# Stick-breaking attention from running sums of weights, with masks on TensorE and a later forget gate

## The chip, the cores and the metric

One core of a Trainium2 chip runs the whole layer. The metric is the device time of one execution in microseconds. TensorE (PE) multiplies matrices, VectorE (DVE) and ScalarE (ACT) work element by element and read PSUM, GpSimd (POOL) works on SBUF and issues a few DMAs, and SyncE (SP) issues the loads.

## What is computed

One decoder layer for 512 tokens of width 1024 in float32: adaLN modulation, an input projection, two attention branches of 8 heads (head dimension 64) on the same input, gated merge, output projection, LayerNorm, then an MLP with a causal convolution and a second LayerNorm. The part that matters here:

```python
def _stick_breaking_attention(q, k, v):
    ...
        z = jnp.einsum('bhqd,bhkd->bhqk', qi, k).astype(jnp.float32) * ATTN_SCALE
        strict = kpos[None, :] < qpos[:, None]
        log_beta = jax.nn.log_sigmoid(z)
        log_one_minus = jnp.where(strict, jax.nn.log_sigmoid(-z), 0.0)
        rest = lax.cumsum(log_one_minus, axis=3, reverse=True) - log_one_minus
        a = jnp.where(strict, jnp.exp(log_beta + rest), 0.0)
        return jnp.einsum('bhqk,bhkd->bhqd', a.astype(v.dtype), v)
...
        log_f = jax.nn.log_sigmoid((f_a + b_forget).astype(jnp.float32)).transpose(0, 2, 1)
```

So the weight of key s for query t is A[t,s] = sigmoid(z[t,s]) times the product of sigmoid(-z[t,j]) over s < j < t, and zero for s >= t. The forgetting branch is a softmax with the running sum of log_f added to the scores.

## The kernel before

Every float32 operand of a matmul is split into a high part (`hi_of`, an ACT copy that rounds, line 75) and a low part (`lo_of`, a DVE subtraction, line 78), and every product is three matmuls of 128 x 512 (lines 116 to 118, 270, 411 to 413, 428 to 430).

The first stage, up to about 50 us, streams w_ada and the first columns of w_in and leaves q and k of the first pair of stick-breaking heads, the first gates and the forget logits in PSUM. `forget_evac` takes the logits out at once; `forget` later makes their log-sigmoid (Abs, Exp, Ln on ACT, lines 324 to 326), sums it with a scan on DVE (line 328), splits it into `chi` and sends rows of it by POOL DMAs into the score operands `s2` and `m2` of the forgetting heads (`decay_rows`, lines 342 and 343).

The second stage is the attention, which the change edits. A list `stream` holds generators of filler matmuls: projections of q and k for later pairs (`proj`), of v for the stick-breaking heads (`vproj`) and for the forgetting heads (`vgroup`), gates and branch projections. `fill(n)` takes the next n matmuls out of it, `fill_to(mark)` takes them up to a mark, and `lim` says how far they may be taken. Their weights are `items`: SP loads each 512 KB item into one of four `raw` buffers (line 132), two items ahead of use they are split. Between the weights stand the `ada` items (`add_ada`, `ada_proc`): the rest of the modulation, done by DVE alone (lines 561 and 566 for the first eight, line 170 for the later ones); `ada_split` and `ada_sum` (lines 584 and 585) sum groups of them over the partitions with TensorE.

16 heads, the 8 stick-breaking ones first, pass three stages. `stage_a` makes the scores of four query blocks with lines 454 and 455 in three PSUM banks, then the weights; `stage_b` turns the weights with TensorE (line 514) and splits them into `ph` and `pl`; `stage_c` multiplies them with v (line 532). Step n of the loop runs stage_a of head n+2, stage_b of head n+1 and stage_c of head n, with 9 filler matmuls between each. Before an even n the q and k projections of the next pair are taken in full; `q_evac` and `k_evac` take them out of PSUM into s1, s2, m1 and m2. Before n = 6 the marks make the four v groups and the projections of pair 4 run in one row. For a forgetting head, stage_a adds the mask `mska` to the diagonal blocks with a matmul (line 460). For a stick-breaking head, ACT makes `om` = sigmoid(-z) and `pt` = sigmoid(z) (lines 487 and 488), POOL sets the masked part of pt to zero (line 490), DVE scans the running product of om from the right, held at 1 in the masked part by the constant `one` (line 493), and POOL multiplies pt by it (line 494).

The instructions of each engine but SP are put in order when the program is built, by a planner that follows the written order as a priority, puts ready work ahead of work that its own cost model has waiting, and hands out the buffers; `tc.issue_after` adds an order on one engine. At run time each engine follows its order. Later stages (output projection, LayerNorm, MLP) are not edited.

Of the kernel before, what the change touches and what calls it, by code (L numbers as in the profile page):

```python
# [45 lines left out]
def layer_kernel(ctx: ExitStack, tc: tile.TileContext, out, xT, x, cT, crow, wa0, wa1, bcol, bgt, w1, wct, wv, bf,  # L46
# [21 lines left out]
    def const(shape, dt, s):  # L68
        return cons.tile(shape, dt, name=s, tag=s)
# [32 lines left out]
    G.memset(zerob, 0.0)  # L102
    mska = const([P, P], BF16, "mska")
    G.affine_select(mska, zerob, pattern=[[-1, P]], compare_op=ALU.is_ge, fill=NEG, base=0, channel_multiplier=1)
    one = const([P, 512], F32, "one")
    G.memset(one, 0.0)
    G.affine_select(one[:, 384:512], one[:, 384:512], pattern=[[-1, P]], compare_op=ALU.is_gt, fill=1.0, base=0, channel_multiplier=1)
    bfs = const([NH, 1], F32, "bfs")
    modc = const([P, 4, KT], F32, "modc")
    modr = const([P, 4, KT, 2], F32, "modr")  # L110
# [29 lines left out]
    def process():  # L140
        it = items[state["proc"]]
        if state["proc"] < EARLY:
            with tc.issue_after(state["after"].ins):
                it[4] = it[1](it[3])
        else:
            it[4] = it[1](it[3])
        state["proc"] += 1
# [208 lines left out]
    def q_evac(br, p, ps):  # L356
        for hh in range(2):
            h = 2 * p + hh
            r = slice(64 * hh, 64 * hh + 64)
            s1 = z(F32R, "s1")  # L360
            hi_of(s1[0:64, :], ps[r, :], 0.125)
            V.scalar_tensor_tensor(s1[64:128, :], ps[r, :], 0.125, fl(s1[0:64, :]), ALU.mult, ALU.subtract)
            d = hd.setdefault((br, h), {})
            d["s1"] = s1
            if br == 0:
                s2 = s2t[slot_free(idx(br, h))]
                hi_of(s2[0:64, :], ps[r, :], 0.125)
                d["s2"] = s2
            else:
                d["s2"] = s1  # L370

    def k_evac(br, p, ps):
        for hh in range(2):
            h = 2 * p + hh
            r = slice(64 * hh, 64 * hh + 64)
            m1 = z(F32R, "m1")
            hi_of(m1[0:64, :], ps[r, :])
            hi_of(m1[64:128, :], ps[r, :])
            m2 = m2t[slot_free(idx(br, h))]
            lo_of(m2[0:64, :], ps[r, :], m1[0:64, :])  # L380
            d = hd.setdefault((br, h), {})
            d["m1"], d["m2"] = m1, m2

    def v_evac(br, j, half, ps):
        vv = z(F32R, "vv")
# [19 lines left out]
    def vproj(br, j, last):  # L405
        ps = bank()
        weights(last)
        tb = slice(j * P, (j + 1) * P)
        for k in range(KT):
            h, l = items[wvi[k // 2]][4][k % 2]  # L410
            PE.matmul(ps, uh[k][:, tb], h, start=k == 0, stop=False)
            PE.matmul(ps, uh[k][:, tb], l, start=False, stop=False)
            PE.matmul(ps, ul[k][:, tb], h, start=False, stop=k == KT - 1)
            yield 3
        for half in range(2):
            v_evac(br, j, half, ps)

    vbk = []

# [25 lines left out]

    def stage_a(br, h):
        d = hd[(br, h)]
        bk = [bank(), bank(), bank()]

        def scores(i):  # L450
            b, o = OFS[i]
            w = max(256, (i + 1) * P)
            tb = slice(i * P, (i + 1) * P)
            PE.matmul(bk[b][:, o : o + w], d["s1"][:, tb], d["m1"][:, 0:w], start=True, stop=False)  # L454
            PE.matmul(bk[b][:, o : o + w], d["s2"][0:68, tb], d["m2"][0:68, 0:w], start=False, stop=br == 1)

        def mask(i):
            b, o = OFS[i]
            if br == 0:
                PE.matmul(bk[b][:, o + i * P : o + i * P + P], identb, mska, start=False, stop=True)  # L460

        scores(0)
        mask(0)
# [19 lines left out]
        else:  # L483
            for b in (0, 2, 1):
                w = SEG[b][-1][1]
                om = z(F32, "om")
                S.activation(om[:, 0:w], bk[b][:, 0:w], AF.Sigmoid, scale=-1.0)
                d["last"] = S.activation(pt[b][:, 0:w], bk[b][:, 0:w], AF.Sigmoid)
                dg = pt[b].rearrange("p (a c) -> p a c", c=P)[:, (0, 3, 1)[b] : w // P : 3, :]
                G.affine_select(dg, dg, pattern=[[0, dg.shape[1]], [-1, P]], compare_op=ALU.is_gt, fill=0.0, base=0, channel_multiplier=1)  # L490
                for s, e in SEG[b]:
                    d0 = om[:, s + 1 : e][:, ::-1]
                    V.tensor_tensor_scan(d0, d0, one[:, 513 - (e - s) : 512][:, ::-1], 1.0, ALU.mult, ALU.max)  # L493
                    G.tensor_tensor(pt[b][:, s : e - 1], pt[b][:, s : e - 1], om[:, s + 1 : e], ALU.mult)  # L494
        d["pt"] = pt
        scored.add(idx(br, h))
        if br == 0 and h + 4 < NH:
# [139 lines left out]
    stream, sums = [], []  # L637
    adas = [0]

    skip = [7]  # L640

    def add_ada(n=1):
        for _ in range(n):
# [42 lines left out]
    for p, ng in ((1, 0), (2, 0), (3, 2), (4, 1)):  # L686
        if p == 4:
            marks["v0"] = len(stream)
            for j in range(4):
                stream.append((vgroup, (j, add_item(wv[0, j], split_proc))))  # L690
                add_ada(2)
        add_pair(p)
        if p == 1:
            for j in range(4):
# [86 lines left out]
    heads = [(br, 2 * p + e) for br, p in seq for e in range(2)]  # L781
    last = hd[heads[1]]['last']
    for n, (b, h) in enumerate(heads):
        if n == 4:
            forget(last)
        f1, f2, f3 = FILL[n // 8]
        if n + 2 < 16:
# [9 lines left out]
        fill(f2)  # L797
        if n == 0:
            fill_to(marks["v1"])
        stage_c(b, h)  # L800
        if n == 7:
            lim[0] = marks["y0"]
# [291 lines left out]
```

## Time and profile before

| | |
|---|---|
| runs (us) | 770.62, 772.75, 772.47; median 772.47 |
| profiled execution | 773.12 us, its span 771.4 us |
| mean granted TensorE clock | 0.994 |
| busy | PE 98%, DVE 71%, ACT 45%, POOL 26% of the span |
| attention | about 50 to 310 us of the span, its stick-breaking heads up to about 200 us |

A row of a timeline gives the start in us, the length in us, the engine, the line of the kernel, the operation and its tiles as out<-in with the shape, and in brackets the idle time of the engine before it with what ended it. A row of a group of instructions gives their count, their busy time in us, the mean ns of one, and the idle time before them. Matmuls overlap: the step from one 512-column matmul to the next is 0.23 us though each shows 0.39.

### The profile page before, as it was taken

The page shows a single profiled execution, that of the slowest core. Times are in us where ns is not written, and L with a number is a line of the kernel's source. Part 1 is how long each engine was busy: PE and PEld are TensorE (multiplying, and loading weights), DVE is VectorE, ACT ScalarE, POOL GpSimd, SP SyncE. Part 2 cuts the span into 40 slices and gives each one's busy share as a digit, 9 for nine tenths or more (in the row PEclk, how much of TensorE's full clock was granted, in tenths as well). Part 3 has the DMA queues.
Part 4 walks back from the last instruction along what each step waited for, and adds up shares of the span by engine and source line. Part 5 has one row for each costly group of instructions (what it writes and reads, how often), then busy time and mean ns, then how long its engine had stood idle before and what let it go on. Part 6 is the DMA issues. An engine that isn't in the chain of part 4 may idle for free.

```text
span 771.4 us, 9543 instructions
## 1 busy us (share of the span) xinstructions
PE 752.7 (98%) x3538; PEld 622.3 (81%) x3538; DVE 546.5 (71%) x816; ACT 350.9 (45%) x587; POOL 197.9 (26%) x162
## 2 busy tenths in 40 slices
PE   8999999898999999999999999999999999999995
PEld 4877888786888888888889888888888888888885
DVE  6868668988789885776676787677656665534666
ACT  3568468725867555433145434444444433222300
POOL 1037236920100011363000780000000043945500
PEclk9999999999999999999999999999999999999999
DMA  8952310378332323455302524344332214322302
GB/s 330 405 181 82 110 56 28 111 243 274 112 113 92 121 86 123 155 166 163 137 1 71 204 76 146 119 178 137 112 106 93 100 54 165 122 96 88 105 27 83
DMA packets 31106, 99.68 MB, mean 129 GB/s; under 512 B 4274, under 2 KB 4786, under 8 KB 31059
## 3 DMA queue, kind: packets, MB, share of 16 engines
q1 hardware_dynamic: 30258, 98.72, 37.3%
q8 instruction: 28, 0.46, 0.3%
q10 hardware_dynamic: 288, 0.28, 0.1%
q0 software_dynamic: 512, 0.07, 0.1%
q14 instruction: 20, 0.16, 0.1%
HBM read 96.88 MB, written 2.10 MB: 128 GB/s over the span
## 4 chain that ended last, share of the span: by engine, by line
PE 83%; DVE 7%; ACT 5%; DMA 3%; issue 2%; DVEq 0%; ACTq 0%
PE ps L116 16%; PE ps L117 16%; PE ps L118 16%; PE ps L985 5%; PE ps L986 5%; PE ps L984 5%; PE ps L270 4%; PE ps L532 2%; PE ps L864 2%; PE ps L863 2%; PE ps L865 2%; PE ps L514 2%; DVE wl L78 1%; PE ps L454 1%; DVE om L493 1%
## 5 line engine op out<-in xcount | busy, mean ns | idle before, releaser
L78 DVE TENSOR_TENSOR wl<-raw,wh 128x1024 fp32r<-128x1024 f32 (+2 forms) x106 | 147.1, 1389 | 92.4 <-ACT wh L75 91.9
L75 ACT ACTIVATE wh<-raw 128x1024 fp32r<-128x1024 f32 (+2 forms) x106 | 110.3, 1042 | 98.7 <-PE ps L986 38.3
L116 PE MATMUL ps<-u2h,wh 128*128 128x512 f32 (+1 forms) x376 | 141.4, 376 | 0.0
L117 PE MATMUL ps<-u2l,wh 128*128 128x512 f32 (+1 forms) x376 | 141.3, 376 | 0.0
L118 PE MATMUL ps<-u2h,wl 128*128 128x512 f32 (+1 forms) x376 | 141.3, 376 | 0.0
L624 POOL TENSOR_TENSOR raw<-raw,gt 128x1024 f32<-128x1024 f32 x22 | 59.7, 2727 | 190.8 <-DVE gt L587 157.7
L117 PEld LDWEIGHTS ps<-u2l,wh 128*128 128x128 f32 x376 | 70.8, 188 | 12.9
L116 PEld LDWEIGHTS ps<-u2h,wh 128*128 128x128 f32 x376 | 70.8, 188 | 12.8
L118 PEld LDWEIGHTS ps<-u2h,wl 128*128 128x128 f32 x376 | 70.8, 188 | 12.6
L116 PE MATMUL ps<-uh,wh 128*128 128x512 f32 x200 | 79.7, 399 | 0.0
L117 PE MATMUL ps<-ul,wh 128*128 128x512 f32 x200 | 78.5, 392 | 0.0
L118 PE MATMUL ps<-uh,wl 128*128 128x512 f32 x200 | 78.4, 392 | 0.0
L985 PE MATMUL ps<-wl,hh 128*128 128x512 f32 x128 | 49.9, 390 | 0.0
L986 PE MATMUL ps<-wh,hl 128*128 128x512 f32 x128 | 49.8, 389 | 0.0
L984 PE MATMUL ps<-wh,hh 128*128 128x512 f32 x128 | 49.8, 389 | 0.0
L118 PEld LDWEIGHTS ps<-uh,wl 128*128 128x128 f32 x200 | 37.7, 189 | 8.1
L116 PEld LDWEIGHTS ps<-uh,wh 128*128 128x128 f32 x200 | 37.8, 189 | 7.1
L117 PEld LDWEIGHTS ps<-ul,wh 128*128 128x128 f32 x200 | 37.9, 189 | 6.9
L75 ACT ACTIVATE hh<-cv 128x512 fp32r<-128x512 f32 x22 | 13.9, 632 | 59.8 <-DVE cv L964 59.8
L612 POOL TENSOR_TENSOR raw<-raw,gt 128x1024 f32<-128x1024 f32 x8 | 19.9, 2498 | 78.2 <-DMA raw<-in_wo 47.2
L963 ACT ACTIVATE cv<-cv 128x512 f32<-128x512 f32 x22 | 13.9, 632 | 54.6 <-DVE cv L958 54.6
L494 POOL TENSOR_TENSOR pt<-pt,om 128x127 f32<-128x127 f32 (+3 forms) x32 | 34.5, 1088 | 1.8
(192 smaller groups left out, 1532.3 us busy)
## 6 DMA issues: line engine op xcount, KB each, us to landing
raw<-in_wup SPq DMA_DIRECT2D x44, 512.0 KB, 3.3
raw<-in_wa SPq DMA_DIRECT2D x32, 512.0 KB, 3.4
raw<-in_wct SPq DMA_DIRECT2D x25, 512.0 KB, 4.0
raw<-in_wdn SPq DMA_DIRECT2D x22, 512.0 KB, 3.3
wa<-in_wa SPq DMA_DIRECT2D x14, 512.0 KB, 7.9
raw<-in_wv SPq DMA_DIRECT2D x8, 512.0 KB, 3.9
raw<-in_wp SPq DMA_DIRECT2D x8, 512.0 KB, 3.4
raw<-in_wo SPq DMA_DIRECT2D x8, 512.0 KB, 3.2
```

Of the source, the lines that this page charges most:

```text
L75: S.activation(o, i, AF.Copy, scale=scale)
L78: return V.tensor_tensor(o, i, fl(hi), ALU.subtract)
L116: PE.matmul(ps, wh, ah, start=first, stop=False)
L117: PE.matmul(ps, wh, al, start=False, stop=False)
L118: PE.matmul(ps, wl, ah, start=False, stop=last)
L270: PE.matmul(grp[g], w, u, start=j == 0 and n == 0, stop=j == KT - 1 and n == (1 if g == 7 else 2))
L494: G.tensor_tensor(pt[b][:, s : e - 1], pt[b][:, s : e - 1], om[:, s + 1 : e], ALU.mult)
L612: G.tensor_tensor(r, r, gt[0], ALU.mult)
L624: G.tensor_tensor(r, r, gt[1], ALU.mult)
L984: PE.matmul(ps, hh[j][:, tb], w[0], start=first, stop=False)
L985: PE.matmul(ps, hh[j][:, tb], w[1], start=False, stop=False)
L986: PE.matmul(ps, hl[j][:, tb], w[0], start=False, stop=last)
```

## The change

The sum of A[t,s] v[s] over s is summed by parts. With R[t,s] the sum of the weights from s to t, it equals the sum over s of R[t,s] (v[s] - v[s-1]), v[-1] being zero. R comes from one scan from the right, R[s] = sigmoid(-z[s]) R[s+1] + sigmoid(z[s]), which is written into pt. The masked part gets its zero weights from TensorE, which adds -1e30 to the diagonal scores. POOL's masking and product of the stick-breaking heads are dropped.

- `v_diff` takes a block of v out of PSUM, shifts it down by one row with POOL DMAs (the row across the blocks alone, the other 127 together), subtracts, and splits the difference.
- `q_evac` and `k_evac` do the high parts of both heads first, then the low parts of both.
- The second weight split of the attention stage follows the low parts of k on each engine, no longer the last split of the first stage.
- The ada items start after two skipped places in place of seven, and one in place of two stands at each v group.
- `forget` is written at n = 6, not 4; 15 filler matmuls more stand before stage_c of head 0.

```diff
@@ -102,9 +102,8 @@
     G.memset(zerob, 0.0)
     mska = const([P, P], BF16, "mska")
     G.affine_select(mska, zerob, pattern=[[-1, P]], compare_op=ALU.is_ge, fill=NEG, base=0, channel_multiplier=1)
-    one = const([P, 512], F32, "one")
-    G.memset(one, 0.0)
-    G.affine_select(one[:, 384:512], one[:, 384:512], pattern=[[-1, P]], compare_op=ALU.is_gt, fill=1.0, base=0, channel_multiplier=1)
+    mskb = const([P, P], BF16, "mskb")
+    G.affine_select(mskb, zerob, pattern=[[-1, P]], compare_op=ALU.is_gt, fill=NEG, base=0, channel_multiplier=1)
     bfs = const([NH, 1], F32, "bfs")
     modc = const([P, 4, KT], F32, "modc")
     modr = const([P, 4, KT, 2], F32, "modr")
@@ -140,7 +139,7 @@
     def process():
         it = items[state["proc"]]
         if state["proc"] < EARLY:
-            with tc.issue_after(state["after"].ins):
+            with tc.issue_after(state["k" if state["proc"] else "after"].ins):
                 it[4] = it[1](it[3])
         else:
             it[4] = it[1](it[3])
@@ -359,7 +358,6 @@
             r = slice(64 * hh, 64 * hh + 64)
             s1 = z(F32R, "s1")
             hi_of(s1[0:64, :], ps[r, :], 0.125)
-            V.scalar_tensor_tensor(s1[64:128, :], ps[r, :], 0.125, fl(s1[0:64, :]), ALU.mult, ALU.subtract)
             d = hd.setdefault((br, h), {})
             d["s1"] = s1
             if br == 0:
@@ -368,6 +366,10 @@
                 d["s2"] = s2
             else:
                 d["s2"] = s1
+        for hh in range(2):
+            r = slice(64 * hh, 64 * hh + 64)
+            s1 = hd[(br, 2 * p + hh)]["s1"]
+            V.scalar_tensor_tensor(s1[64:128, :], ps[r, :], 0.125, fl(s1[0:64, :]), ALU.mult, ALU.subtract)
 
     def k_evac(br, p, ps):
         for hh in range(2):
@@ -376,10 +378,27 @@
             m1 = z(F32R, "m1")
             hi_of(m1[0:64, :], ps[r, :])
             hi_of(m1[64:128, :], ps[r, :])
-            m2 = m2t[slot_free(idx(br, h))]
-            lo_of(m2[0:64, :], ps[r, :], m1[0:64, :])
             d = hd.setdefault((br, h), {})
-            d["m1"], d["m2"] = m1, m2
+            d["m1"], d["m2"] = m1, m2t[slot_free(idx(br, h))]
+        for hh in range(2):
+            r = slice(64 * hh, 64 * hh + 64)
+            d = hd[(br, 2 * p + hh)]
+            state["k"] = lo_of(d["m2"][0:64, :], ps[r, :], d["m1"][0:64, :])
+
+    vfs = []
+
+    def v_diff(j, ps):
+        vf, dv = z(F32, "vf"), z(F32, "dv")
+        S.activation(vf, ps, AF.Copy)
+        if j == 0:
+            G.memset(dv[0:1, :], 0.0)
+        else:
+            G.dma_start(dv[0:1, :], vfs[-1][P - 1 : P, :])
+        G.dma_start(dv[1:P, :], vf[0 : P - 1, :])
+        vfs.append(vf)
+        V.tensor_tensor(dv, vf, dv, ALU.subtract)
+        for half in range(2):
+            v_evac(1, j, half, dv)
 
     def v_evac(br, j, half, ps):
         vv = z(F32R, "vv")
@@ -412,8 +431,7 @@
             PE.matmul(ps, uh[k][:, tb], l, start=False, stop=False)
             PE.matmul(ps, ul[k][:, tb], h, start=False, stop=k == KT - 1)
             yield 3
-        for half in range(2):
-            v_evac(br, j, half, ps)
+        v_diff(j, ps)
 
     vbk = []
 
@@ -445,6 +463,7 @@
 
     def stage_a(br, h):
         d = hd[(br, h)]
+        msk = mska if br == 0 else mskb
         bk = [bank(), bank(), bank()]
 
         def scores(i):
@@ -452,12 +471,11 @@
             w = max(256, (i + 1) * P)
             tb = slice(i * P, (i + 1) * P)
             PE.matmul(bk[b][:, o : o + w], d["s1"][:, tb], d["m1"][:, 0:w], start=True, stop=False)
-            PE.matmul(bk[b][:, o : o + w], d["s2"][0:68, tb], d["m2"][0:68, 0:w], start=False, stop=br == 1)
+            PE.matmul(bk[b][:, o : o + w], d["s2"][0:68, tb], d["m2"][0:68, 0:w], start=False, stop=False)
 
         def mask(i):
             b, o = OFS[i]
-            if br == 0:
-                PE.matmul(bk[b][:, o + i * P : o + i * P + P], identb, mska, start=False, stop=True)
+            PE.matmul(bk[b][:, o + i * P : o + i * P + P], identb, msk, start=False, stop=True)
 
         scores(0)
         mask(0)
@@ -486,12 +504,9 @@
                 om = z(F32, "om")
                 S.activation(om[:, 0:w], bk[b][:, 0:w], AF.Sigmoid, scale=-1.0)
                 d["last"] = S.activation(pt[b][:, 0:w], bk[b][:, 0:w], AF.Sigmoid)
-                dg = pt[b].rearrange("p (a c) -> p a c", c=P)[:, (0, 3, 1)[b] : w // P : 3, :]
-                G.affine_select(dg, dg, pattern=[[0, dg.shape[1]], [-1, P]], compare_op=ALU.is_gt, fill=0.0, base=0, channel_multiplier=1)
                 for s, e in SEG[b]:
-                    d0 = om[:, s + 1 : e][:, ::-1]
-                    V.tensor_tensor_scan(d0, d0, one[:, 513 - (e - s) : 512][:, ::-1], 1.0, ALU.mult, ALU.max)
-                    G.tensor_tensor(pt[b][:, s : e - 1], pt[b][:, s : e - 1], om[:, s + 1 : e], ALU.mult)
+                    q0 = pt[b][:, s:e][:, ::-1]
+                    V.tensor_tensor_scan(q0, om[:, s:e][:, ::-1], q0, 0.0, ALU.mult, ALU.add)
         d["pt"] = pt
         scored.add(idx(br, h))
         if br == 0 and h + 4 < NH:
@@ -637,7 +652,7 @@
     stream, sums = [], []
     adas = [0]
 
-    skip = [7]
+    skip = [2]
 
     def add_ada(n=1):
         for _ in range(n):
@@ -688,7 +703,7 @@
             marks["v0"] = len(stream)
             for j in range(4):
                 stream.append((vgroup, (j, add_item(wv[0, j], split_proc))))
-                add_ada(2)
+                add_ada()
         add_pair(p)
         if p == 1:
             for j in range(4):
@@ -781,7 +796,7 @@
     heads = [(br, 2 * p + e) for br, p in seq for e in range(2)]
     last = hd[heads[1]]['last']
     for n, (b, h) in enumerate(heads):
-        if n == 4:
+        if n == 6:
             forget(last)
         f1, f2, f3 = FILL[n // 8]
         if n + 2 < 16:
@@ -797,6 +812,7 @@
         fill(f2)
         if n == 0:
             fill_to(marks["v1"])
+            fill(15)
         stage_c(b, h)
         if n == 7:
             lim[0] = marks["y0"]
```

## The prediction

> **What bounds the kernel now.** I read the page's busy times first.
>
> ```profile
> span 771.4 us, 9543 instructions
> ## 1 busy us (share of the span) xinstructions
> PE 752.7 (98%) x3538; PEld 622.3 (81%) x3538; DVE 546.5 (71%) x816; ACT 350.9 (45%) x587; POOL 197.9 (26%) x162
> ```
>
> TensorE is busy 752.7 of 771.4 us. So the change can gain only where PE waits or runs slowly, and every matmul that it adds costs. Second, the waits of PE (total us, times, longest):
>
> ```profile
> PE ps L454 <- ACT m L75: 4.1, 2, 2.1
> PE ps L163 <- DMA cbr<-in_crow: 2.2, 1, 2.2
> PE ps L585 <- DVE acl L78: 1.1, 1, 1.1
> PE ps L412 <- DVE wvl L78: 1.0, 1, 1.0
> PE ps L428 <- DVE pl L78: 1.0, 1, 1.0
> ```
>
> L163 stands in the first microseconds, which the change leaves alone. In the attention part PE waits for ACT and DVE; the three smaller rows left out don't name POOL either. The largest wait is that of the score matmuls (L454) for the evacuated k (tile m). Third, the busy times by stretch, around these waits (the first three) and over the stretches that the change loads and unloads:
>
> ```profile
> 66.00:76.00 10.00, 8.53 (x40) 6.13 (x40) 7.96 (x11) 6.51 (x12) 6.93 (x8) 1.00 0.31 105
> 133.00:142.00 9.00, 6.90 (x32) 5.79 (x31) 7.41 (x12) 5.76 (x12) 7.66 (x12) 0.81 0.39 120
> 185.00:196.00 11.00, 7.97 (x31) 5.71 (x29) 8.79 (x15) 5.76 (x10) 0.00 (x0) 0.84 0.70 220
> 95.00:135.00 40.00, 39.67 (x205) 33.38 (x203) 30.30 (x41) 29.46 (x53) 19.55 (x23) 1.00 0.12 41
> 160.00:185.00 25.00, 25.00 (x112) 20.64 (x111) 19.86 (x36) 7.61 (x14) 0.00 (x0) 1.00 0.85 284
> ```
>
> Columns: stretch, length, PE, PEld, DVE, ACT, POOL busy, granted PE clock, DMA share, GB/s. A wait costs more than its length: in 133:142 PE idles 2.1 us and has a clock of 0.81, which loses another 9.0 x 0.19 = 1.7. In 185:196 it idles 3.0 and loses 11.0 x 0.16 = 1.8. Together with 1.5 us idle in 66:76 and the 1.0 us at L428, 11.1 us stand to be won. That is the ceiling.
>
> [...]
>
> **The change part by part.** The profiled execution took 773.12 us, its span of 771.4 and 1.7 around it; the median of the three runs is 772.47. I sum against 773.12 and carry the difference to the median.
>
> *POOL's work goes.* These are the two groups that vanish, then the scan at its widest, and the one multiply-and-add scan that the trace has (count | busy, mean ns | idle before):
>
> ```profile
> L494 POOL TENSOR_TENSOR pt<-pt,om 128x127 f32<-128x127 f32 (+3 forms) x32 | 34.5, 1088 | 1.8
> L490 POOL TENSOR_SCALAR_AFFINE_SELECT pt<-pt 128x128 f32<-128x128 f32 (+1 forms) x24 | 20.1, 840 | 28.9 <-ACT pt L488 28.8
> ```
>
> ```profile
> L493 DVE TENSOR_TENSOR_SCAN om<-om,one 128x511 f32<-128x511 f32 x8 | 10.4, 1294 | 0.0
> ```
>
> ```profile
> L328 DVE TENSOR_TENSOR_SCAN fq<-ones,fq 8x512 f32<-8x512 f32 x1 | 1.2, 1210 | 0.0
> ```
>
> 54.6 us leave POOL, but PE never waited for them: worth 0 by itself. What hid them is the matmul fill between the stages of a head; it stays. The scan keeps its count and grows by one column; multiply-and-add took 1210 ns for 512 columns against 1294 for 511 now, so I price it at no change.
>
> *Masks on TensorE.* Four 128-column matmuls for each of 8 stick-breaking heads. The first pair of rows frames the scores of such a head without them, the second those of a forgetting head, which has them already:
>
> ```profile
> 121.19 0.28 PE L454 MATMUL ps<-m,s 128*128 128x256 f32 x1
> ...
> 122.73 0.40 PE L117 MATMUL ps<-ul,wh 128*128 128x512 f32 x1
> ```
>
> ```profile
> 229.58 0.28 PE L454 MATMUL ps<-m,s 128*128 128x256 f32 x1
> ...
> 231.48 0.39 PE L117 MATMUL ps<-ul,wh 128*128 128x512 f32 x1
> ```
>
> From the first score matmul to the second filler behind: 1.54 us without, 1.90 with. 0.36 x 8 = **+2.9 us**, on the path, uncovered.
>
> *Forget gate from head 4 to head 6.* On ACT it is three table loads, of which the first and the last stand here, and four activations like the one shown:
>
> ```profile
> 118.95 1.28 ACT L325 ACT_TABLE_LOAD   x1
> 120.25 0.63 ACT L325 ACTIVATE fq<-fq 8x512 f32<-8x512 f32 x1
> ...
> 125.65 1.28 ACT L487 ACT_TABLE_LOAD   x1
> ```
>
> That is 3 x 1.28 + 4 x 0.63 = 6.4 us, in front of the sigmoids of head 5 and the q and k evacuation of pair 3; on DVE the 1.2 us scan and two operations beside it, which I put at half of it each, 2.4. Then PE waits for m:
>
> ```profile
> 136.77 0.82 PE L454 MATMUL ps<-m,s 128*128 128x256 f32 x3 [2.10 <-ACT m L75]
> ```
>
> Moved, forget runs beside the v and pair-4 projections (144 matmuls in a row), with ACT busy 7.6 of 25 us in 160:185. Its POOL DMAs go along and must land before the first forgetting head, whose scores follow the wait near 190. Of the 3.8 us I take **-3.3**: the evacuation itself (four ACT copies, two DVE subtractions) can still be late by some tenths.
>
> *The ada items, five places earlier* (skip 7 to 2) and one instead of two per v group. Up to head 6, DVE gets about six more of them and 160:195 loses five. An early item is two of these:
>
> ```profile
> L566 DVE SCALAR_TENSOR_TENSOR ac<-raw,cTs,ac 128x512 f32<-128x512 f32 x28 | 23.4, 835 | 1.6 <-DMA raw<-in_wa 1.3
> ```
>
> In 185:196 DVE works 8.8 of 11 us, and acl and the evacuation of pair 4 stand behind ada work. With the ada_split now at the first v group, the 1.1 us wait for acl goes whole; of the wait for m with its slow clock (3.8) I take two thirds: **-3.6** in all. The price is in 95:135: four items x 1.67 = 6.7 us come, forget's 2.4 goes, so DVE goes from 30.3 to about 34.6 of some 38 us (fill(15) takes 3.4 us of matmuls out, masks bring 1.1). It is not full, but queues get longer: **+0.3**, bounds 0 and 3.8 (the whole wait of 133:142 again). Each item is a 512 KB load on SP's queue; in 95:135 the DMA share is 0.12, so they fit, and 160:185 with 0.85 is relieved.
>
> *The k and q evacuations* now do all ACT copies before the DVE subtractions:
>
> ```profile
> L75 ACT ACTIVATE m<-ps x20: 572/592/595, 52.9 to 195.6; 64x512 fp32r<-64x512 f32 x20
> L78 DVE TENSOR_TENSOR m<-ps,m x10: 673/688/693, 54.1 to 197.3; 64x512 fp32r<-64x512 f32 x10
> ```
>
> (Columns: ns min/median/max, first and last start.) The first head's m2 comes two copies later, 1.18 us; the second head's stays where it was, since four copies and two subtractions, 3.7 us, are in line either way. Fill matmuls stand ready around the scores, so **+0.5**; bounds 0 and 7 pairs x 1.18 = 8.3. At the start one weight split on DVE moves behind the k evacuation, so head 0 begins earlier by its length and DVE clears the queue that ended the waits of 66:76 sooner: **-1.0** of 1.5. The 1.0 us at L428 waits for pl, a subtraction in DVE's queue, which loses work there: **-0.5**.
>
> *Differences of v.* Per block of 128 keys: an ACT copy, a subtraction, and a POOL DMA that shifts 127 rows of 2 KB down by one. Only the last block matters; the heads' fill covers the others. The rows nearest to its steps:
>
> ```profile
> L595 ACT ACTIVATE sg<-ps 128x512 f32<-128x512 f32 x16 | 9.2, 615 | 1.3 <-PE ps L270 1.2
> ```
>
> ```profile
> s<-chi POOLq DMA_DIRECT2D x4, 4.0 KB, 2.4
> ```
>
> ```profile
> GB/s 330 405 181 82 110 56 28 111 243 274 112 113 92 121 86 123 155 166 163 137 1 71 204 76 146 119 178 137 112 106 93 100 54 165 122 96 88 105 27 83
> ```
>
> ```profile
> L964 DVE TENSOR_TENSOR cv<-cv,cv 128x512 f32<-128x512 f32 x22 | 17.1, 777 | 0.9
> ```
>
> ```profile
> L75 ACT ACTIVATE vv<-ps x8: 383/384/459, 80.9 to 95.5; 128x256 fp32r<-128x256 f32 x8
> L78 DVE TENSOR_TENSOR vv<-ps,vv x8: 393/425/427, 81.3 to 95.9; 128x256 fp32r<-128x256 f32 x8
> ```
>
> ```profile
> 94.20 0.39 PE L413 MATMUL ps<-wvh,ul 128*128 128x512 f32 x1
> ...
> 95.11 0.56 PE L532 MATMUL ps<-ph,vv 128*128 128x512 f32 x2
> ```
>
> Copy 0.62; landing 2.4 (median from issue, for 4 KB) plus 260 KB at the best rate of the page, 405 GB/s, 0.64; subtraction 0.78; split 0.38 + 0.42: 5.2 us from the last v matmul. Before stage_c stood 3 matmuls (94.20 to 95.11 is four steps, 0.228 each); with fill(15) there are 18, or 4.1 us. The rest is a wait of **+1.1**; bounds 0 (the planner puts more filler ahead) and 10.8 (the transfer on one engine, below). While ACT and DVE wait for a landing, the sigmoids and scans of heads 2 and 3 queue behind.
>
> Sum: -3.3 - 3.6 - 1.0 - 0.5 = -8.4; +2.9 + 0.3 + 0.5 + 1.1 = +4.8; together -3.6. 773.12 - 3.6 = 769.5, and from the median **768.9 us**.
>
> **Rivals.** [...]
>
> [...]
>
> *No change: the wait stays, with a new cause.* DVE, at nine tenths in 95:135, takes the ada items where forget was, and PE waits for m again: -3.3 and half of the -3.6 are lost, 774.0. For it: pl, s and m stand behind those items in DVE's queue. Against: ACT, which loses 6.4 us there, is the engine that PE's waits name.
>
> *All waits go.* The 11.1 us are won, and only the masks are paid: -8.2, 764.3. Against it: an evacuation chain of about 3.7 us stands ahead of each pair's scores in any case.
>
> *The headline does nothing:* POOL's removal is worth 0 here already; only the moves count.
>
> **Numbers.** Chances: forecast 0.53, of which 0.14 ends within 0.3% (2.3 us, about what a measurement of this kernel can tell from no change); all waits go 0.15; no change 0.18 (0.08 same, 0.10 slower); one engine 0.14. Faster 0.54, same 0.22, slower 0.24. The forecast's own range is 765.5 to 772.5. The range to hold 8 in 10 goes from 763.5 to 776.0; it leaves out the one-engine case and a little below.
>
> **What would show it.** L490 and L494 gone, and 64 mask matmuls in place of 32, with about 1.9 us per stick-breaking score stage. The forget table loads after 145 us. No PE wait for m near 135, clock near 1.0 in 133:142; a shorter wait near 190. Wrong if L532's first wait for vv is over 2 us, if dv's DMA lands later than 6 us, if DVE fills 95:135 and waits for m remain, or if L455 waits for the late m2.

## The result and the profile after

The changed kernel took 776.8 us (median of 6 runs, 775.55 to 777.93) against 772.61 us of the kernel before on the same chip: a ratio of 1.0047, 95% interval [1.0029, 1.0065]. It is slower by 4.2 us, where 3.6 us less were predicted, and lies above the upper end of the range, 776.0. The profiled execution took 776.09 us.

The busy times of its page, then PE's waits (total us, times, longest):

```profile
span 774.3 us, 9546 instructions
PE 754.7 (97%) x3570; PEld 622.2 (80%) x3570; DVE 541.6 (70%) x820; ACT 354.6 (46%) x592; POOL 146.2 (19%) x113
```

```profile
PE ps L547 <- DVE vv L78: 3.2, 1, 3.2
PE ps L162 <- DMA cbr<-in_crow: 2.4, 1, 2.4
PE ps L446 <- DVE pl L78: 1.6, 1, 1.6
PE ps L473 <- ACT m L75: 1.5, 3, 0.8
```

POOL lost 51.7 us of work. The waits for k's evacuation (m) shrank from 4.1 to 1.5 us, and a new wait of 3.2 us for the split differences of v stands at the top, at the first `stage_c` (L547). The wait for pl at the start of the v group (L428 before, L446 now) grew from 1.0 to 1.6. The same stretches as before, with two more (columns as in the prediction):

```profile
66.00:76.00 10.00, 9.98 (x50) 8.11 (x49) 8.18 (x13) 7.78 (x13) 0.00 (x0) 1.00 0.40 146
133.00:142.00 9.00, 9.00 (x53) 7.62 (x52) 8.42 (x13) 6.62 (x12) 0.52 (x1) 1.00 0.17 61
185.00:196.00 11.00, 10.85 (x49) 8.66 (x48) 8.11 (x14) 7.32 (x13) 0.00 (x0) 1.00 0.64 220
95.00:135.00 40.00, 35.87 (x184) 29.38 (x183) 27.09 (x42) 25.85 (x52) 2.62 (x5) 0.96 0.21 68
98.00:103.00 5.00, 1.77 (x9) 1.22 (x8) 1.45 (x3) 1.21 (x3) 1.00 (x2) 1.00 0.21 52
103.00:108.00 5.00, 5.00 (x22) 4.06 (x20) 2.25 (x4) 1.78 (x3) 0.54 (x1) 0.66 0.30 73
```

The three stretches that the prediction wanted to mend are mended, idle time and clock both. What it cost stands in 95:135, which was full before: 4.1 us idle, most of it in 98:103, where DVE and ACT are mostly idle too, and then a clock of 0.66.

For the experiments I use one more number. The **excess** of a stretch is what PE took in it beyond full speed (512 columns in 0.228 us, as in the prediction's 94.20 to 95.11), idle time and slow clock together, added up over the starts of its matmuls in the trace:

```
us         66:80  80:110  133:145  145:180  180:200  235:300
before       3.1     1.3      4.6      1.9      6.1      4.3
after        1.1     6.6      1.4      3.7      1.8      5.2
```

So 66:80, 133:145 and 180:200 gave 9.5 us; 80:110 and 145:180 took 7.1 back, 110:133 (1.6 before, 3.3 after) another 1.7 and 235:300 another 0.9, and the 32 new mask matmuls come on top.

### The profile page after: what moved, and what is told of

Read it like the earlier page. It is cut to its first block, busy times and chain, and to the rows that moved or that the text cites. A ratio compares the mean times of both kernels' runs of the same rounds, so it can differ in the third digit from the quotient of the medians.

```text
span 774.3 us, 9546 instructions
## 1 busy us (share of the span) xinstructions
PE 754.7 (97%) x3570; PEld 622.2 (80%) x3570; DVE 541.6 (70%) x820; ACT 354.6 (46%) x592; POOL 146.2 (19%) x113
## 4 chain that ended last, share of the span: by engine, by line
PE 80%; DVE 8%; issue 5%; ACT 4%; DMA 3%; POOL 0%; DVEq 0%; ACTq 0%; POOLq 0%
PE ps L115 15%; PE ps L116 15%; PE ps L117 15%; PE ps L1000 5%; PE ps L1002 5%; PE ps L1001 5%; PE ps L269 5%; PE ps L880 2%; PE ps L879 2%; PE ps L881 2%; ACT m L75 2%; PE ps L547 1%; DMA dv<-vf 1%; PE ps L473 1%; PE ps L474 1%
## 5 line engine op out<-in xcount | busy, mean ns | idle before, releaser
L78 DVE TENSOR_TENSOR wl<-raw,wh 128x1024 fp32r<-128x1024 f32 (+2 forms) x106 | 146.3, 1380 | 94.2 <-ACT wh L75 93.9
L75 ACT ACTIVATE wh<-raw 128x1024 fp32r<-128x1024 f32 (+2 forms) x106 | 110.1, 1040 | 103.1 <-PE ps L1002 38.4
L75 ACT ACTIVATE hh<-cv 128x512 fp32r<-128x512 f32 x22 | 13.9, 631 | 59.7 <-DVE cv L980 59.7
L973 DVE SCALAR_TENSOR_TENSOR cv<-ps,cw,cv 128x511 f32<-128x511 f32 x44 | 32.7, 742 | 2.3 <-ACT cv L972 2.3
```

The costliest lines, as they stand in the source:

```text
L75: S.activation(o, i, AF.Copy, scale=scale)
L78: return V.tensor_tensor(o, i, fl(hi), ALU.subtract)
L973: V.scalar_tensor_tensor(t[:, 1:], ps[:, 0:511], cw[:, n, 1:2], t[:, 1:], ALU.mult, ALU.add)
```

## Experiments

Each run is one edit, but its instructions are put in order anew when it is built, so an edit can also move work that it doesn't name. Times are medians, traces show one execution each, "over" and "under" are differences from the median of the kernel before, run beside it on the same chip, and the ratio follows with its interval. The "side edits" are all but the sums by parts: the q and k evacuation order with the early split, the ada items, forget at head 6.

**1. The change in halves.** Four runs: v taken as it is, which leaves out copy, shift and subtraction (`a_nodiff`); no mask matmuls in the stick-breaking heads, which leaves their later keys in (`a_nomask`); the kernel before with the side edits alone (`b_side`); the changed kernel with the side edits undone (`b_parts`).

```
a_nodiff   -        v_diff(j, ps)
           +        for half in range(2):
           +            v_evac(1, j, half, ps)
a_nomask   +            if br == 0:
                            PE.matmul(bk[b][...], identb, msk, ...)
b_side     before, with the hunks of process, q_evac, k_evac, skip, add_ada() and n == 6
b_parts    after, with those same hunks taken back
```

> The kernel after, with v taken as it is: no copy, no shift, no subtraction (leaves out the differences of v). Theory V, the chain of the differences is what made the change lose: ACT waits for each shift with the next block's copy queued behind it, PE waits 3.2 us at the first head's last product and then runs at half clock, 5.3 us in 80:110; about 771.5 us, and no wait of L547 in 95:110. Rival E, masks and the new evacuation order lose it: at most 1 us better, about 776.

> The kernel after without the mask matmuls of the stick-breaking heads (leaves out their masking). Both theories: the masks are on the path at 0.36 us a head, 2.9 us in all, about 773.9. If they hide in time that PE waits anyway, about 776.5.

> The kernel before with the side edits alone: forget at n = 6, ada items earlier, both heads' high parts first, the second split behind the k evacuation; POOL masks and multiplies as before. Theory V: these edits win what the traces show in 66:80, 133:142 and 180:198 (2.0 + 3.7 + 4.6 us) less what waits for the late m2 cost (about 3): some 766. Rival E: the evacuation order and the moved forget gate cost as much as they give, 770 to 774.

> The kernel after with the side edits undone: sums by parts, masks and fill(15), but forget at n = 4, ada items late, old evacuation order. Theory V: before plus 2.9 for masks plus 5.3 for the differences, about 780.5, with the wait near 135 still there. Rival E: about 774 to 776.

- a_nodiff: 769.67 us, 2.8 under before, 0.9965 [0.9948, 0.9983]. The differences of v cost 7.0 us (4.2 + 2.8), where the prediction had 1.1.
- a_nomask: 776.7, 4.2 over, 1.006 [1.0035, 1.0084]: no gain from taking the masks out.
- b_side: 772.12, 0.35 under, 0.9993 [0.9975, 1.001]: the side edits together win nothing that can be measured, where 7.6 were predicted.
- b_parts: 777.62, 5.2 over, 1.007 [1.0049, 1.009].

Two steps of the sum are wrong, then: the differences of v, and something among the side edits. They hardly touch each other, since the sums by parts cost 5.2 us without the side edits and 4.5 with them.

**2. Who waits for the shift.** ACT in the changed kernel, around the idle time of PE (start, us, instruction, and in brackets the idle time before it and what ended that):

```profile
95.60 0.72 ACT L75 ACTIVATE vv<-dv 128x256 fp32r<-128x256 f32 x2 [4.14 <-DVE dv L399]
96.23 0.96 ACT L75 ACTIVATE ph<-ps 128x512 fp32r<-128x512 f32 x2
97.08 0.60 ACT L392 ACTIVATE vf<-ps 128x512 f32<-128x512 f32 x1
101.64 0.72 ACT L75 ACTIVATE vv<-dv 128x256 fp32r<-128x256 f32 x2 [3.96 <-DVE dv L399]
102.26 0.58 ACT L392 ACTIVATE vf<-ps 128x512 f32<-128x512 f32 x1
```

The copies of blocks 2 and 3 (L392) start at 97.08 and 102.26, each behind the split of the block before (L75, vv), which waited some 4 us for that block's shift. The four chains run one after the other instead of overlapped: copy, DMA, subtraction, split, and only then the next copy. The tile's own view, and the DMA view of 80:104:

```profile
DVE dv L399: 15.6, 4
DMA dv<-vf: 6.6, 3
DMA to landing us min/median/max: 2.4/3.4/7.2
```

```profile
dv<-vf POOLq DMA_DIRECT2D x4, 254.0 KB, 3.1
```

ACT idled 15.6 us for the four blocks. The shift itself takes 3.1 us from issue to landing (median), close to the prediction's 3.0 (2.4 + 0.64). So the test is to keep every instruction and change only the order, and beside it to test forget's place:

```
a_fix    -        S.activation(vf, ps, AF.Copy)
         +        cp = S.activation(vf, ps, AF.Copy)
         ...
         -        V.tensor_tensor(dv, vf, dv, ALU.subtract)
         -        for half in range(2):
         -            v_evac(1, j, half, dv)
         +        vds.append(dv)
         +        for i in ([j - 1] if j else []) + ([j] if j == NB - 1 else []):
         +            V.tensor_tensor(vds[i], vfs[i], vds[i], ALU.subtract)
         +            with tc.issue_after(cp.ins):
         +                for half in range(2):
         +                    v_evac(1, i, half, vds[i])
a_f7     -            forget(last)
         +            forget(hd[heads[7]]["last"])
a_fixf7  both;   b_side7  b_side with the edit of a_f7
```

> The changed kernel with v_diff in two phases: subtraction and splits of block j are written, and ordered by issue_after, behind the ACT copy of block j+1. Same work, same DMAs. Theory (ACT's order is the cost: each copy of v stands behind the previous block's wait for its shift): the last copy comes at about 95 us in place of 102.3, the splits are ready before PE asks for them, the wait of 3.2 us at stage_c and the slow clock behind it go: 770 to 772. Rival 1 (the shift's landing itself, or the added ACT and DVE work, is the cost, whatever the order): a wait for vv of 2 us or more stays, 775 to 777.

> The changed kernel with forget ordered behind the last sigmoid of head 7 in place of head 6's; nothing else. Theory (the scheduler pulls forget's table loads in front of head 7's sigmoids, so pl is late at the start of the v group and PE waits 1.6 + 0.5 us for banks and splits): that wait goes, 774 to 775. Rival (the decay rows then come too late for the first forgetting heads, or PE waits for pl anyway because of DVE's queue): 776 to 779.

> Both edits, the two-phase v_diff and forget behind head 7's sigmoids. Theory (two independent waits): the gains add, 768 to 770, below the kernel before. Rival (both gains are eaten by the next late evacuation, as the removal of the masks was): 772 to 775.

> The kernel before with the side edits alone (q and k evacuation order, early split, ada items, forget late), and forget ordered behind head 7's sigmoids. Theory (the side edits do win what was predicted near 70, 135 and 190, but forget in front of head 7's sigmoids gives it back as 3.5 us of wait for pl at the v group's start and a slow clock): without it 766 to 769. Rival (that wait comes from DVE's queue of ada items, not from forget): 771 to 773, with the wait for pl still above 2 us.

- a_fix: 771.24, 1.9 under before, 0.997 [0.9952, 0.9989].
- a_f7: 777.51, 4.4 over, 1.0062 [1.0037, 1.0086].
- a_fixf7: 772.5, 0.6 under, 0.9979 [0.9958, 1.0].
- b_side7: 772.44, 0.7 under, 0.9983 [0.9967, 0.9999].

The order alone takes back 6.1 of the 7.0 us. ACT of a_fix, and its PE wait for vv:

```profile
89.15 0.60 ACT L392 ACTIVATE vf<-ps 128x512 f32<-128x512 f32 x1
91.77 0.73 ACT L75 ACTIVATE vv<-dv 128x256 fp32r<-128x256 f32 x2 [2.03 <-DVE dv L401]
94.59 0.60 ACT L392 ACTIVATE vf<-ps 128x512 f32<-128x512 f32 x1 [2.09 <-PE ps L435]
95.10 0.72 ACT L75 ACTIVATE vv<-dv 128x256 fp32r<-128x256 f32 x2
99.14 0.73 ACT L75 ACTIVATE vv<-dv 128x256 fp32r<-128x256 f32 x2 [3.31 <-DVE dv L401]
```

```profile
PE ps L550 <- DVE vv L78: 0.2, 1, 0.2
```

The last copy now waits for PE's last v matmul (L435), not for a shift, and comes 7.7 us earlier; the wait of 3.2 is 0.2, and the excess of 80:110 is 2.0. The shifts were no faster here (4.2 us from issue to landing at the median of all seven, against 3.4 in the changed kernel), so the rival, the shift as such, falls and the theory is shown. The order doesn't always take the whole wait away: the traces of later runs with the same order have 0.8 to 2.1 us of it, most in a_fixf7_adaoldk.

Forget's place is the other way round. In a_f7 (its trace is its fastest execution, 774.16) the wait for pl at the v group is down to 0.5, as the theory had it, but one of 2.4 us comes at the first forgetting head, the excess of 180:200 goes from 1.8 to 5.9, and the time doesn't move. b_side7 and a_fixf7 show the same trade (8.7 and 7.1 in 180:200). What the forgetting head waits for is seen in a_fixf7, on PE and on DVE:

```profile
193.67 0.36 PE L477 MATMUL ps<-m,s 68*128 68x256 f32 x1 [3.22 <-issue]
```

```profile
191.62 1.23 DVE L169 SCALAR_TENSOR_TENSOR raw<-raw,cbc 128x1024 f32<-128x1024 f32 x1 [1.94 <-DMA raw<-in_wa]
192.78 0.08 DVE L169 DVE_READ_ACCUMULATOR raw<-raw,cbc 128x1 f32 x1
192.89 1.41 DVE L78 TENSOR_TENSOR m<-ps,m 64x512 fp32r<-64x512 f32 x2
```

The profile names no releaser for L477, but the first of the two late halves of k (m, L78) ends where it starts. DVE had been idle for 1.94 us before that, standing at an ada item whose load hadn't landed, with the late halves behind it. That is the picture of ACT and the shift again, on another engine.

**3. The ada items.** Three of them are moved out of DVE's way, the old k order is tried with that, the masks are taken out again without the wait for v, and the ada edits are put on the kernel before by themselves.

```
a_fixf7_ada       a_fixf7, and in the loop over the v groups, ahead of add_ada():
                  +                skip[0] += 3 if j == 3 else 0
a_fixf7_adaoldk   the same, k_evac with lo_of(m2...) inside the first loop, as before
a_fix_nomask      a_fix with the edit of a_nomask
b_ada             before with    -    skip = [7]           +    skip = [2]
                                 -    add_ada(2)           +    add_ada()
```

> The two-phase v_diff with forget behind head 7 (772.5), and no ada item behind the last v group nor beside the two projections of pair 4; the three go to later places. Theory (DVE stands in order before an ada item that waits for its load, and the late half of k stands behind it: 192.9 to 194.2, so the first forgetting head's second score matmul waits 3.2 us and a slow clock follows): the wait of 3.2 us and most of the excess of 7.1 us in 180:200 go, 767 to 769. Rival (forget's rows or the evacuations as such are late there, whatever DVE waits for): a wait of over 2 us stays, 771 to 773.

> The run a_fixf7_ada with the k evacuation in the old order (per head: two ACT copies, then the DVE subtraction). Theory of the prediction (the new order makes the first head's late half about one microsecond later, nothing more): 0 to 1 us faster than a_fixf7_ada. Rival (the new order frees DVE earlier and costs nothing): the same or up to 2 us slower.

> The two-phase v_diff (771.2) with no mask matmuls in the stick-breaking heads, so that their future keys are left unmasked. Theory (the masks cost TensorE's time only, 32 x 57 ns and some load of weights, and where PE doesn't wait that shows): 768 to 770. Rival (as without the two phases, where their removal gained nothing: the time goes into the waits for the evacuations): 771 to 772.

> The kernel before with the ada edits alone (skip 2, one item per v group). The prediction's step: the wait for m near 190 and its slow clock go for the most part, 768 to 770. Rival (loads, not DVE, set when ada items end, and the evacuations still queue behind one that waits): the excess of 6.1 us in 180:200 stays above 4, 772 to 774.

- a_fixf7_ada: 767.53, 4.5 under before, 0.9938 [0.9911, 0.9965].
- a_fixf7_adaoldk: 767.41, 0.994 [0.9921, 0.9959]: the order of k makes no difference there.
- a_fix_nomask: 771.54 beside a_fix's 771.24; 0.9994 [0.9972, 1.0015]: again no gain: beside the kernel before, a_fix is 1.9 under and a_fix_nomask 0.5. PE's waits for vv and wl are 1.6 and 0.9 us in its trace (0.2 and none in a_fix).
- b_ada: 777.28, 5.3 **over** before, 1.0067 [1.004, 1.0094]: slower than both expectations.

In a_fixf7_ada DVE reaches the late halves at 188.95, and PE's wait is 0.5, with an excess of 2.1 in 180:200:

```profile
187.68 1.22 DVE L169 SCALAR_TENSOR_TENSOR raw<-raw,cbc 128x1024 f32<-128x1024 f32 x1 [0.67 <-DMA raw<-in_wa]
188.84 0.08 DVE L169 DVE_READ_ACCUMULATOR raw<-raw,cbc 128x1 f32 x1
188.95 1.41 DVE L78 TENSOR_TENSOR m<-ps,m 64x512 fp32r<-64x512 f32 x2
```

**4. Each side edit alone, and the sums by parts in a mended order.**

```
a_best        a_fixf7_ada once more
b_side7_ada   b_side7 with the skip of a_fixf7_ada
b_evac        before with the hunks of process, q_evac and k_evac
b_forget6     before with    -        if n == 4:          +        if n == 6:
```

> The kernel of a_fixf7_ada once more (two-phase v_diff, forget behind head 7's sigmoids, three ada items away from the last v group and pair 4), to compare with b_side7_ada on one chip: 767 to 769, below the kernel before by 0.4 to 0.7%.

> The kernel before (products of a scan, with POOL) with the same side edits and orders as a_best. Theory (the sums by parts are worth nothing in themselves, and with the shift out of ACT's way cost nothing; b_side7 and a_fixf7 stood at 772.4 and 772.5): within 1 us of a_best. Rival (without POOL's 54.6 us the heads end sooner, which shows once the other waits are gone): a_best is faster by 2 us or more. Second rival (the masks' price of 2.9 shows now): a_best is slower by 2 us or more.

> The kernel before with the q and k evacuation order and the early split alone. The prediction's terms: +0.5 - 1.0, so 772. Rival (with all four copies ahead, ACT no longer stands behind DVE's queue, so the waits for m near 135 and 190 shorten): 769 to 771.

> The kernel before with forget at head 6 alone. The prediction's step: -3.3, so 769. Rival (the scheduler runs it in front of head 7's sigmoids, and the wait moves from 137 to the v group's start): 771 to 774, with PE waiting over 2 us for pl there.

- a_best: 767.09, 5.8 under, 0.9934 [0.9913, 0.9955]. b_side7_ada: 766.27, 6.6 under, 0.9916 [0.9899, 0.9932]. The intervals overlap: with the orders mended, products on POOL and sums by parts can't be told apart. The profiled execution of a_best, the slowest of its six at 771.39, has the wait of the forgetting head again, 2.0 us with an excess of 5.0 in 180:200, so a_fixf7_ada's trace is not how every execution of that kernel goes.
- b_evac: 770.04, 2.9 under, 0.9962 [0.9947, 0.9977]; 0.5 was predicted, and the rival's figure came.
- b_forget6: 770.56, 2.35 under, 0.9967 [0.9955, 0.9978]; 3.3 was predicted.

**5. The two that gain, without the one that loses.**

```
b_evacforget   b_evac with    -        if n == 4:          +        if n == 6:
b_ada_lull     b_ada with the skip of a_fixf7_ada
```

> The kernel before with the evacuation order, the early split and forget at head 6; the ada items as they were. Theory (the gains of 2.9 and 2.3 add, and the ada edits alone gave them back): 767 to 768.5. Rival (both shorten the same waits, so together they give little more than one): 769.5 to 771.

> The kernel before with the ada edits, and the three items behind the last v group and beside pair 4 moved to later places. Theory (their cost is that DVE stands in order before an item whose load is late, with the evacuations of pair 4 behind it): the wait for m of 4.5 us near 190 goes, 771 to 773.5. Rival (the cost lies elsewhere, as in the wait for m near 271): 775 to 778.

- b_evacforget: **765.92**, 6.5 under before, 0.99 [0.9879, 0.9922]. It has nothing of the sums by parts and is the fastest kernel of the study by its median; the intervals of b_side7_ada and a_best overlap with its own.
- b_ada_lull: 772.25, 0.2 under, 0.9991 [0.9974, 1.0009]: the 5 us that the ada edits cost are those of the three items.

PE's wait for m near 190, in b_ada, then in b_ada_lull:

```profile
192.93 1.05 PE L454 MATMUL ps<-m,s 128*128 128x256 f32 x3 [4.47 <-ACT m L75]
```

```profile
190.68 0.74 PE L454 MATMUL ps<-m,s 128*128 128x256 f32 x3 [1.72 <-ACT m L75]
```

Near 190 is not the only place. Of b_ada's excess over before, 180:200 has 1.0 us (7.1 against 6.1) and 235:300 has 3.7 (8.0 against 4.3). There DVE stands before an item's load again, k's low part comes late, and PE waits for it and then runs at a clock of 0.51 in 275.0 to 278.5. First DVE, then PE:

```profile
269.75 1.23 DVE L170 SCALAR_TENSOR_TENSOR raw<-raw,cbc 128x1024 f32<-128x1024 f32 x1 [2.47 <-DMA raw<-in_wa]
```

```profile
273.50 0.38 PE L455 MATMUL ps<-m,s 68*128 68x256 f32 x1 [1.71 <-DVE m L78]
```

In b_ada_lull the two stretches have 2.9 and 5.3.

b_side is b_evacforget with the ada edits, and stands 6.2 us above it. Both traces have forget on ACT at the same place (its first activation at 139.40 and 139.32), so what differs there is DVE. First b_side, then b_evacforget (head 7's scans are L498):

```profile
145.41 2.33 DVE L571 SCALAR_TENSOR_TENSOR ac<-raw,cTs,ac 128x512 f32<-128x512 f32 x3
...
150.86 1.19 DVE L170 SCALAR_TENSOR_TENSOR raw<-raw,cbc 128x1024 f32<-128x1024 f32 x1
...
151.98 3.17 DVE L498 TENSOR_TENSOR_SCAN om<-om,one 128x127 f32<-128x127 f32 x4
...
155.74 0.68 DVE L78 TENSOR_TENSOR pl<-ps,ph 128x512 fp32r<-128x512 f32 x1
```

```profile
146.76 0.68 DVE L327 SCALAR_TENSOR_TENSOR fq<-fq,fq 8x512 f32<-8x512 f32 x1 [0.27 <-ACT fq L326]
147.47 1.21 DVE L328 TENSOR_TENSOR_SCAN fq<-ones,fq 8x512 f32<-8x512 f32 x1
148.68 3.29 DVE L498 TENSOR_TENSOR_SCAN om<-om,one 128x127 f32<-128x127 f32 x4
151.89 0.66 DVE L78 TENSOR_TENSOR pl<-ps,ph 128x512 fp32r<-128x512 f32 x1
```

The ada work (L571, L170) stands ahead of head 7's scans and makes them 3.3 us later, pl 3.85 later. PE's first v matmuls need pl's bank: the wait there is 3.55 us in b_side (L433 at 156.47) and 0.4, for another tile, in b_evacforget. In b_ada, with forget still at head 4, 145:180 costs nothing more than before (an excess of 1.6 against 1.9): where the items hurt depends on what else stands in DVE's queue.

## Why the prediction was wrong

**The differences of v: +1.1 predicted, +7.0 measured.** The failing sentence is "Only the last block matters; the heads' fill covers the others". The chain's parts were sized well (copy 0.6, landing 3.1, subtraction 0.69, splits 0.4 each). The prediction even said that ACT and DVE would queue behind a landing, but it counted heads 2 and 3 as what queues there, and not the next block's copy. With that copy in the queue the chains did not overlap, and PE waited already for the splits of block 2: it resumed at 102.56, in the middle of them (DVE's start at 102.08), when block 3's copy had just begun. Of the excess of 80:110, which rose by 5.3 us, 3.2 is this wait and most of the rest the slow clock behind it. a_fix shows it: the same work in another order costs 0.9 us over a_nodiff (with intervals of some 1.4 us on each side), about the size that was predicted.

**The ada items: -3.6 + 0.3 predicted, about +5 measured** (b_ada alone; +6.2 beside the other two side edits). The prediction looked for their price where it expected DVE's added load, in 95:135, and found room. No ada pass (L566 and L170 before, L581 and L169 now) ran there at all, in either kernel, and DVE did 27.1 us and not 34.6: eight passes went ahead of that stretch, into 66:95, and others behind it. What they cost is what a queue costs, not what a share costs: in b_side at 145 to 152, in front of head 7's scans; in b_ada near 190 and near 270, in front of k. Near 190 the step did remove the wait for acl, but an item whose load is late holds DVE while k waits behind it (1.94 us in a_fixf7, 2.47 us near 270 in b_ada). The rival "no change: the wait stays" named DVE, at another place. The -0.5 at L428 falls with it: that wait is for pl, and it grew to 1.6 us.

**Forget: -3.3 predicted, -2.35 measured alone.** The sign and the size held within the interval (0.9955 is 3.5 us); the path didn't. Forget did not move beside the v and pair-4 projections but stands ahead of them. In the changed kernel the planner put all its table loads ahead of head 7's sigmoids (four, where three were priced, since a gate's sigmoid, L610, fell between them); in b_forget6 two of four stand there. So the near match is partly luck. The loads of the changed kernel:

```profile
147.66 1.28 ACT L324 ACT_TABLE_LOAD   x1
149.61 1.28 ACT L610 ACT_TABLE_LOAD   x1
152.14 1.28 ACT L325 ACT_TABLE_LOAD   x1
154.08 1.28 ACT L505 ACT_TABLE_LOAD   x1
```

Pushing it behind those sigmoids gained nothing as long as DVE was late near 190 (a_f7, b_side7).

**The evacuations and the early split: +0.5 - 1.0 predicted, -2.9 measured.** Mis-sized. The second head's half was taken to stay where it was because its copies stand in line either way. In the old order they don't only stand in line: in the trace of before, ACT's second copy of q waits for DVE's subtraction (2.06 us of ACT idle at 188.05), and DVE may be at something else. With all four copies in front that wait is gone. The excess of 66:80 fell by 1.4 in b_evac and that of 133:145 by 1.7. The price that was predicted came too, and larger than 0.5: PE waits 2.5 us for the late m2 in that trace, which is the slowest of its seven executions, and 145:180 takes 2.4 back. b_evac bundles the orders of q and k and the early split; which of them gains is not shown, and a_fixf7_adaoldk, with the old order of k, was no slower. With forget moved as well the gain is 6.5, more than the 5.2 of both alone; whether that surplus is real can't be said within the intervals.

**The masks: +2.9 predicted, none measured.** The score stage did lengthen as it was sized, to 1.90 us (at 129.29 and 149.65 in the changed kernel), but beside the kernel before, taking the masks out changed 4.2 over into 4.2 over and 1.9 under into 0.5 under. By the intervals each of these comparisons is good to about 2.3 us, so a price of 2.9 is excluded and a small one isn't. The working counted them as uncovered because PE executes them; it left out that PE stands waiting for ACT and DVE a little later, and gets there sooner without them. In a_fix_nomask the waits for vv and wl are longer (1.6 and 0.9 us, where a_fix has 0.2 and none); that the time went just there is read from single executions and not shown.

**What held.** POOL's 54.6 us were predicted to be worth nothing, and with the orders mended nothing can be measured (a_best 767.09, b_side7_ada 766.27). The multiply-and-add scan costs no more than the old one (1201 ns for 512 columns against 1294 for 511). The waits near 135 and 66:76 went. The wait near 190 went too, but in the changed kernel PE came there late, at 195.0; in a_f7 and a_fixf7, which brought it sooner, there was a wait again.

**The rivals.** No run shows the transfer on one engine, which the prediction has at 10.8 us as the bound of the wait and at a chance of 0.14: four shifts of 254 KB landed 3.1 us after their issue at the median, and PE's wait was 3.2. Only the first took 7.2; why, the runs don't show. The test that the prediction set for itself was the right one: a first wait for vv of over 2 us. It came with 3.2, from a cause that no rival named. The second test, a landing later than 6 us, was met by the first shift alone (7.2 us; the longest in a_fix took 6.6, and PE's wait for vv was 0.2 there), so it said nothing of the cost.

The sum with measured terms: evacuations and forget together -6.5, the ada items +6.2 (b_side over b_evacforget), the sums by parts on top +4.5 (after over b_side), of which the differences of v are 7.0 and the rest is -2.5: +4.2, the measured result. These are steps from one kernel to the next, so they add up by construction and confirm nothing. What stays open: the rest of -2.5 (POOL's work, the scan, the masks and fill(15) together) was not taken apart; and the changed kernel with a_fix and the ada items as they were before was not run, and whether it would beat 765.9 is not known.

## What to carry to other kernels

Here one instruction's wait for a DMA became the wait of all that stood behind it on its engine (ACT idled 15.6 us for four shifts, DVE 1.94 us for one load): before adding a chain "copy, DMA, use" to a loop, write down what stands behind the use on its engine, and put the next round's copy ahead of it. Price a moved work item by what queues behind it at the place where it lands, and by when its data lands; the engine's busy share over a long stretch says nothing of either. Keep PE's waits apart as well as short: in these traces no window of 3.41 us of which PE idled a share of up to 0.46 was followed by a slow clock, and each one over 0.56 was (3.41 us at 0.50, which lose another 1.7 us). When several edits are bundled, price each alone on the kernel before: here two of the small ones were worth 6.5 us, a third cost as much, and the headline cost 4.5 until its order was mended, and then nothing that could be measured.

## What the hardware showed that was not expected

ACT and DVE kept their order through the waits shown above: 15.6 us of ACT idle at the splits of the changed kernel, with a copy behind each of the first three, and 1.94 us (a_fixf7) and 2.47 us (b_ada) of DVE idle at an ada item, with the late halves of k behind it.

The slow clock does not follow from a wait's length alone. Two waits of PE in a_fix, of 1.78 and 1.87 us:

```profile
154.76 0.50 PE L449 MATMUL ps<-wh,uh 128*128 128x512 f32 x1 [1.78 <-DVE pl L78]
```

```profile
194.43 0.36 PE L477 MATMUL ps<-m,s 68*128 68x256 f32 x1 [1.87 <-issue]
```

The shorter one was followed by a slow clock (0.50), the longer was not (1.00). What sets them apart in the traces is where the wait lies. In the traces of this case the slow stretches within an execution are 3.41 us long, or twice that, and all changes of the granted clock lie a whole number of 3.41 us apart (in the kernel before it is slow from 137.29 and from 191.90, which is 16 times 3.41 later). Counted off in windows of 3.41 us from such a change, these are the windows of a_fix around the two waits (PE's busy time stands first, the granted clock before the DMA share):

```profile
152.88:156.29 3.41, 1.63 (x8) 1.26 (x8) 3.38 (x7) 3.36 (x5) 0.00 (x0) 1.00 0.02 5
156.29:159.71 3.42, 3.42 (x10) 2.65 (x9) 3.39 (x5) 0.89 (x2) 3.18 (x7) 0.50 0.16 31
190.43:193.84 3.41, 2.13 (x15) 1.55 (x13) 1.43 (x3) 2.01 (x3) 0.00 (x0) 1.00 0.54 173
193.84:197.25 3.41, 2.82 (x16) 2.38 (x17) 3.33 (x8) 1.26 (x6) 1.01 (x2) 1.00 0.48 157
```

The first wait lies in one window, of which PE idles 1.78 us, a share of 0.52; the second is cut by a window's edge into shares of 0.37 and 0.17. The twenty traces (before, after and the runs) have 4401 full-speed windows between the first one and the end of the matmuls. Where PE idled for a share of up to 0.46, none was followed by a slow one; over 0.56, all 13 were (0.61 and 0.57 in the kernel before, 0.60 at the wait of 3.23 us in the changed kernel); between, 5 of 16.
